# Stick-breaking attention in a hybrid trunk: VectorE and GpSimd swap the token tiles that they multiply, and the three passes of the value product change places

## The chip, the cores and the metric

The kernel runs on one core of one Trainium2 chip. The metric is the device time of one execution in microseconds. The kernel before was timed in three runs: 2732.86 us is the median, 2730.51 us the fastest and 2734.73 us the slowest. The profile comes from one further execution, with a time of its own.

The engines are named as in the profile: PE is TensorE's matmuls, PEld its weight loads, DVE is VectorE, ACT ScalarE, POOL GpSimd, and SP the queue that issues most transfers. L545 is line 545 of the kernel.

## The reference

One layer of a decoder is computed for 2048 tokens of width 1024, with 16 learned tokens put in front. The normed input is projected to some 9,200 columns. Three mixers with 4 heads of 128 read these: a stick-breaking attention, a gated delta rule and a gated linear recurrence (HGRN2). Each mixer's output is gated, projected back, gated again and summed; an output projection and the residual follow. The change touches the attention only:

```python
z = einsum('bhqd,bhkd->bhqk', q, k) * scale
log_keep = where(mask, log_sigmoid(-z), 0.0)
log_passed = cumsum(log_keep, axis=3, reverse=True) - log_keep
attn = where(mask, exp(log_sigmoid(z) + log_passed), 0.0)
out = einsum('bhqk,bhkd->bhqd', attn, v)
```

A key's weight is thus the sigmoid of its score, times the product, over all keys between it and the query, of the sigmoids of the negated scores. That running product, taken from the newest key back to the oldest, is what the kernel calls the remainder.

## The kernel before, in words

The sequence is cut into four quarters (j = 0 to 3) of 512 tokens, and a quarter into four token tiles (i = 0 to 3) of 128. For each quarter there is dense work (projections, branch products, output projection: `dense_work`) and there are scans (the attention head by head in `sb_scan`, then the delta rule in `gdn_mats` and `gdn_scan`, then HGRN2 in `hg_scan`). A matrix product in fp32 precision is split in three: both operands are held as a high part and a low part, and `mm3` (L175) adds three passes in PSUM, high by high, high by low, low by high (L176, L177, L178). One such pass over 512 columns is one MATMUL.

`weave` (L1427) runs a scan and the dense work as two generators and takes steps from one and the other by fixed numbers of microseconds. That sets the order in which the program is written. The framework's own scheduler (`schedule_with_timeline_sim`, L1610) then sets the final order on each engine from its estimate of times, so a change in one place can shift the order of other instructions. Each engine runs its instructions strictly in that order, and waits on semaphores.

The attention of one head and one quarter works down the keys' blocks, newest first, in two generators that `alternate`.

- `weights` (L519) goes through the four token tiles. For each: three passes on PE give the scores z; ACT takes two sigmoids (L533, the remainder's factor `pc`; L534, the weight's factor `at`); POOL sets or copies one column (L536, L538); DVE forms the running product with a TENSOR_TENSOR_SCAN (L539); and L545 multiplies `at` by `pc`. The engine of L545 alternates: tiles 0 and 2 on DVE, tiles 1 and 3 on POOL.
- `values` (L549) takes the finished block: PE transposes the products of all four tiles (L567) into one PSUM tile, ACT copies that as the high part `ath` (L578; L572 and L574 for the 16 learned tokens), DVE subtracts to get the low part `atl` (L127, a helper that other code uses as well), and `product` (L551) adds three passes into the accumulator `av`: values high by weights high, values high by weights low, values low by weights high. For the learned tokens it is one pass (L556).

At the end of a head `put_ob` (L407, L410) multiplies by the gate and splits the result. Most small tiles come from one ring of 21 buffers called S, so a buffer's next use waits for the last reader of its earlier use. The saved keys and values of older quarters are loaded through SP (L601 to L606), on the queue that loads weights too (L149).

The delta rule's products (L864), its block inverse on DVE (L923, L928), a transpose (L936) and its small matmuls on PE (L952, L973, L976) follow the attention of a quarter. Lines after L558 stand three lower in the changed file: L567 is L570 there, and L952 is L955.

Of the kernel before, what the change touches and what calls it, by code (L numbers as in the profile page):

```python
# [39 lines left out]
def kernel(  # L40
# [21 lines left out]
    nc = tc.nc  # L62
# [21 lines left out]
    def slot(tag, shape=(P, WQ), dt=F32, bufs=None):  # L84
        return pool.tile(list(shape), dt, tag=tag, name=nm(tag), bufs=bufs or BUFS[tag])
# [18 lines left out]
    def p_z():  # L104
        return ps_z.tile([P, 512], F32, tag="z", name=nm("z"))

    def p_tr():
        return ps_z.tile([P, 512], F32, tag="z", name=nm("tr"))

    def p_av():  # L110
        return ps_av.tile([P, 512], F32, tag="av", name=nm("av"))
# [14 lines left out]
    def sub_lo(out_, a, hi, eng=None):  # L126
        (eng or nc.gpsimd).tensor_sub(out_, a, hi.bitcast(F32))  # L127
# [47 lines left out]
    def mm3(dst, lh, ll, rh, rl, first, last):  # L175
        nc.tensor.matmul(dst, lh, rh, start=first, stop=False)  # L176
        nc.tensor.matmul(dst, lh, rl, start=False, stop=False)  # L177
        nc.tensor.matmul(dst, ll, rh, start=False, stop=last)  # L178
# [226 lines left out]
    def put_ob(src_ps, gate):  # L405
        t = slot("S")
        nc.vector.tensor_mul(t[:, META:], src_ps, gate[:, META:])  # L407
        oh = slot("ob", (P, TQ), F32R)
        ol = slot("ob", (P, TQ), F32R)
        nc.scalar.copy(oh, t[:, META:])  # L410
        sub_lo(ol, t[:, META:], oh)
        return oh, ol
# [99 lines left out]
    def sb_scan(j, h, st):  # L512

        qh, ql, kh, kl, vh, vl, vm0, rq, gate = st.pop(h)
        av = p_av()
        carry = [None] * NT
        started = [False]

        def weights(s, lo, hi, skh, skl, ats):  # L519
            for i in range(NT):  # L520
                e = min(hi, META + (i + 1) * P) if s == j else hi
                if e <= lo:
                    continue
                n = e - lo
                z = p_z()
                diag = s == j and e == META + (i + 1) * P
                qs = slice(META + i * P, META + (i + 1) * P)
                mm3(z[:, :n], qh[:, qs], ql[:, qs], skh[:, lo:e], skl[:, lo:e], True, not diag)
                if diag:
                    nc.tensor.matmul(z[:, n - P : n], ident_b, neg_b, start=False, stop=True)  # L530
                pc = slot("S")
                at = slot("S")
                nc.scalar.activation(pc[:, :n], z[:, :n], AF.Sigmoid, scale=rq[:, NT + i : NT + i + 1])  # L533
                nc.scalar.activation(at[:, :n], z[:, :n], AF.Sigmoid, scale=rq[:, i : i + 1])  # L534
                if carry[i] is None:
                    nc.gpsimd.memset(pc[:, n : n + 1], 1.0)  # L536
                else:
                    nc.gpsimd.tensor_copy(pc[:, n : n + 1], carry[i][:, 0:1])  # L538
                nc.vector.tensor_tensor_scan(  # L539
                    pc[:, 0:n][:, ::-1], pc[:, 0:n][:, ::-1], zero1.broadcast_to([P, n]),  # L540
                    1.0 if carry[i] is None else pc[:, n : n + 1], ALU.mult, ALU.add,
                )
                carry[i] = pc
                eng = nc.gpsimd if i % 2 else nc.vector
                eng.tensor_mul(at[:, :n], at[:, :n], pc[:, 1 : n + 1])  # L545
                ats[i] = at
                yield 0.4 + n * 0.0045

        def values(s, work, svh, svl, vm, final):  # L549
            def product(wi, ath, atl):  # L550
                lo, ats, a, kw, kt = work[wi]  # L551
                cs_ = slice(kt if (s == j and kt is not None) else 0, None)
                cs_ = slice(cs_.start * P, TQ)
                last = final and wi == len(work) - 1
                if kt is None:
                    nc.tensor.matmul(av, vm, ath[:96], start=not started[0], stop=last)  # L556
                else:
                    lh, ll = svh[:, kt * P : (kt + 1) * P], svl[:, kt * P : (kt + 1) * P]  # L558
                    mm3(av[:, cs_], lh, ll, ath[:, cs_], atl[:, cs_], not started[0], last)
                started[0] = True  # L560

            left = None
            for wi, (lo, ats, a, kw, kt) in enumerate(work):
                i0 = kt if (s == j and kt is not None) else 0
                tr = p_tr()
                for i in range(i0, NT):
                    nc.tensor.transpose(tr[:kw, i * P : (i + 1) * P], ats[i][:, a - lo : a - lo + kw], ident)  # L567
                ath = slot("S", (P, TQ), F32R)
                if kt is None:

                    atl = None
                    nc.scalar.copy(ath[:32], tr[:32])  # L572
                    sub_lo(ath[32:64], tr[:32], ath[:32], nc.vector)
                    nc.scalar.copy(ath[64:96], tr[:32])  # L574
                else:
                    atl = slot("S", (P, TQ), F32R)
                    cs_ = slice(i0 * P, TQ)
                    nc.scalar.copy(ath[:, cs_], tr[:, cs_])  # L578
                    sub_lo(atl[:, cs_], tr[:, cs_], ath[:, cs_], nc.vector)
                if left:  # L580
                    product(*left)
                left = (wi, ath, atl)
                yield 0.7
            product(*left)
            yield 0.1

        before = None
        work = []
        for s in range(j, -1, -1):
            vm = vm0  # L590
            if s == j:
                skh, skl, svh, svl = kh, kl, vh, vl
            else:
                cs = 0 if s == 0 else META
                skh = slot("S", dt=F32R)
                skl = slot("S", dt=F32R)
                svh = slot("S", (P, TQ), F32R)
                svl = slot("S", (P, TQ), F32R)
                dd = d_kv[(s, h, "k")] + d_kv[(s, h, "v")]
                for t_, d_ in ((skh, dd[0]), (skl, dd[1])):  # L600
                    nc.sync.dma_start(t_[:, cs:].bitcast(F32), d_[:, cs:])  # L601
                for t_, d_ in ((svh, dd[2]), (svl, dd[3])):
                    nc.sync.dma_start(t_.bitcast(F32), d_)
                if s == 0:
                    vm = slot("vmp", (96, HD), F32R, 2)
                    nc.sync.dma_start(vm.bitcast(F32), dd[4])  # L606
            for lo, hi in [(META + 2 * P, WQ), (0, META + 2 * P)] if s == 0 else [(META, WQ)]:
                ats = {}
                now = weights(s, lo, hi, skh, skl, ats)
                if before is None:  # L610
                    yield from now
                else:
                    yield from alternate(now, before)
                if lo == 0:
                    work.append((lo, ats, 0, 32, None))
                for kt in range(NT):
                    if lo <= META + kt * P < hi:
                        work.append((lo, ats, META + kt * P, P, kt))
                if s == j == 0 and lo > 0:
                    continue  # L620
                if s == j:
                    work.sort(key=lambda w_: -1 if w_[4] == 0 else (0 if w_[4] is None else w_[4]))
                before = values(s, work, svh, svl, vm, lo == 0)
                work = []
        yield from before
        return put_ob(av, gate)
# [708 lines left out]
    def alternate(*gens):  # L1335
        live = list(gens)
        while live:
            for g_ in list(live):
                c = next(g_, None)
                if c is None:  # L1340
                    live.remove(g_)
                else:
                    yield c
# [271 lines left out]
```

## Time and profile before

| | |
|---|---|
| median of three runs | 2732.86 us |
| the profiled execution: its time | 2729.9 us |
| the profiled execution: its span, first to last instruction | 2728.1 us |
| mean granted TensorE clock | 0.999 |
| matmuls, and weight loads | 17984 each |
| L545 on DVE | 108 instructions, median 442 ns |
| L545 on POOL | 108 instructions, median 673 ns |

The span is 1.8 us shorter than the execution's time, and that time is 3.0 us below the median of the three runs. A group in the profile reads: line, engine, operation, output and inputs by name, shape, count, then busy time and mean duration, then the idle time of the engine just before and what ended it. Wait rows give total, number and longest wait in microseconds. Matmuls overlap: each lasts about 0.4 us by the profile's model, but the next one starts 0.23 us after the one before.

### The profile page before, as it was taken

How to read it: one execution, taken by the hardware profiler on the slowest of the kernel's cores; microseconds unless marked ns; L12 is line 12 of the kernel's file. 1: busy time of each engine (PE TensorE's matmuls, PEld its weight loads, DVE VectorE, ACT ScalarE, POOL GpSimd, SP SyncE). 2: the span in 40 equal slices, each digit the busy share in tenths (PEclk: the TensorE clock that was granted, in tenths of full speed). 3: DMA queues.
4: the chain of work that ended last, by engine and by line, in shares of the span. 5: the costliest groups of instructions: out<-in, count | busy, mean ns of one | idle time of the engine just before them, and what ended most of it. 6: DMA issues, size and time to landing. Idle time of an engine off the chain costs nothing.

```text
span 2728.1 us, 46691 instructions
## 1 busy us (share of the span) xinstructions
PE 2690.0 (99%) x17984; PEld 2243.4 (82%) x17984; DVE 1432.5 (53%) x2870; ACT 961.0 (35%) x2199; POOL 717.7 (26%) x989
## 2 busy tenths in 40 slices
PE   7999999999999999999999999999999999999999
PEld 6998888888888888888888888888888887787887
DVE  5476647645357734443255765554325568556422
ACT  5564343343346212212144641321214456313120
POOL 4555213433133401112122332111212223302111
PEclk9999999999999999999999999999999999999999
DMA  7667756679554654557755456355774454554556
GB/s 263 221 234 251 256 178 221 231 268 320 195 180 146 205 177 130 157 158 241 231 190 171 156 168 205 106 158 155 248 221 140 163 168 143 164 161 122 160 163 213
DMA packets 200834, 521.08 MB, mean 191 GB/s; under 512 B 42848, under 2 KB 44832, under 8 KB 200612
## 3 DMA queue, kind: packets, MB, share of 16 engines
q1 hardware_dynamic: 200324, 518.03, 59.0%
q8 instruction: 142, 2.33, 0.3%
q14 instruction: 80, 0.66, 0.1%
q10 hardware_dynamic: 288, 0.07, 0.0%
HBM read 397.57 MB, written 120.44 MB: 190 GB/s over the span
## 4 chain that ended last, share of the span: by engine, by line
PE 92%; DVE 5%; DMA 1%; ACT 1%; issue 1%; POOL 0%; SPq 0%; DVEq 0%; ACTq 0%; POOLq 0%
PE acc L176 20%; PE acc L177 20%; PE acc L178 20%; PE av L176 5%; PE av L177 5%; PE av L178 5%; PE tr L567 2%; PE t L389 2%; PE z L1160 1%; PE z L176 1%; PE z L177 1%; PE z L178 1%; PE z L864 1%; PE tr L389 1%; PE tr L1245 1%
## 5 line engine op out<-in xcount | busy, mean ns | idle before, releaser
L176 PE MATMUL acc<-xh,w 128*128 128x512 f32 (+2 forms) x2096 | 796.8, 380 | 5.6 <-DVE y L1293 1.7
L177 PE MATMUL acc<-xl,w 128*128 128x512 f32 (+2 forms) x2096 | 790.0, 377 | 0.3 <-DVE xl L269 0.2
L178 PE MATMUL acc<-xh,w 128*128 128x512 f32 (+2 forms) x2096 | 786.7, 375 | 0.0
L176 PEld LDWEIGHTS acc<-xh,w 128*128 128x128 f32 x2096 | 396.1, 189 | 75.2 <-DVE y L1293 2.2
L178 PEld LDWEIGHTS acc<-xh,w 128*128 128x128 f32 x2096 | 396.4, 189 | 66.2 <-issue 0.2
L177 PEld LDWEIGHTS acc<-xl,w 128*128 128x128 f32 x2096 | 395.9, 189 | 65.2 <-DVE xl L269 1.3
L539 DVE TENSOR_TENSOR_SCAN S<-S,zero 128x128 f32<-128x128 f32 (+4 forms) x216 | 196.7, 913 | 113.8 <-ACT S L533 107.1
L127 POOL TENSOR_TENSOR w<-wraw,w 128x512 fp32r<-128x512 f32 x106 | 147.3, 1392 | 239.9 <-ACT w L156 222.4
L545 POOL TENSOR_TENSOR S<-S,S 128x256 f32<-128x256 f32 (+2 forms) x108 | 96.5, 894 | 367.1 <-DVE S L539 190.7
L176 PE MATMUL av<-xh,w 128*128 128x512 f32 (+2 forms) x440 | 172.7, 392 | 0.0
L177 PE MATMUL av<-xl,w 128*128 128x512 f32 (+2 forms) x440 | 171.9, 391 | 0.0
L178 PE MATMUL av<-xh,w 128*128 128x512 f32 (+2 forms) x440 | 171.3, 389 | 0.0
L156 ACT CAST w<-wraw 128x512 fp32r<-128x512 f32 x182 | 112.6, 619 | 142.4 <-PE acc L178 70.9
L533 ACT ACTIVATE S<-z,rq 128x128 f32<-128x128 f32 (+4 forms) x216 | 117.3, 543 | 117.7 <-PE z L178 90.2
L745 DVE SCALAR_TENSOR_TENSOR D<-D,cw,D 128x512 f32<-128x512 f32 (+1 forms) x144 | 119.0, 833 | 21.3 <-ACT D L743 19.8
L127 DVE TENSOR_TENSOR S<-tr,S 128x512 fp32r<-128x512 f32 (+4 forms) x176 | 105.9, 607 | 42.7 <-ACT S L572 24.0
L1297 POOL TENSOR_TENSOR y<-y,g 128x512 f32<-128x512 f32 x32 | 48.2, 1507 | 288.9 <-DVE g L1295 288.9
L176 PE MATMUL acc<-ob,w 128*128 128x512 f32 x296 | 118.0, 399 | 1.4 <-ACT ob L410 1.4
L177 PE MATMUL acc<-ob,w 128*128 128x512 f32 x296 | 117.7, 398 | 0.0
L178 PE MATMUL acc<-ob,w 128*128 128x512 f32 x296 | 117.6, 397 | 0.0
L534 ACT ACTIVATE S<-z,rq 128x128 f32<-128x128 f32 (+4 forms) x216 | 117.0, 542 | 0.0
L133 POOL TENSOR_SCALAR nu<-nv 128x8 f32<-128x8 f32 (+3 forms) x39 | 14.8, 379 | 334.2 <-DVE nv L1065 193.6
(407 smaller groups left out, 4978.2 us busy)
## 6 DMA issues: line engine op xcount, KB each, us to landing
w<-wk SPq DMA_DIRECT2D x555, 512.0 KB, 3.7
wk<-w SPq DMA_DIRECT2D x184, 512.0 KB, 3.5
wraw<-in_w_in_dram SPq DMA_DIRECT2D x142, 256.0 KB, 4.0
D<-in_xq_dram SPq DMA_DIRECT2D x56, 256.0 KB, 4.6
S<-rows SPq DMA_DIRECT2D x48, 256.0 KB, 5.2
S<-dv SPq DMA_DIRECT2D x48, 256.0 KB, 4.8
out_dram<-D SPq DMA_DIRECT2D x32, 256.0 KB, 4.6
S<-dk SPq DMA_DIRECT2D x24, 264.0 KB, 3.9
```

What stands on the lines that cost most here:

```text
L127: (eng or nc.gpsimd).tensor_sub(out_, a, hi.bitcast(F32))
L156: nc.scalar.copy(hi, raw)
L176: nc.tensor.matmul(dst, lh, rh, start=first, stop=False)
L177: nc.tensor.matmul(dst, lh, rl, start=False, stop=False)
L178: nc.tensor.matmul(dst, ll, rh, start=False, stop=last)
L389: nc.tensor.transpose(pt[:, n * P : (n + 1) * P], src[:, META + n * P : META + (n + 1) * P], ident)
L533: nc.scalar.activation(pc[:, :n], z[:, :n], AF.Sigmoid, scale=rq[:, NT + i : NT + i + 1])
L534: nc.scalar.activation(at[:, :n], z[:, :n], AF.Sigmoid, scale=rq[:, i : i + 1])
L539: nc.vector.tensor_tensor_scan(pc[:, 0:n][:, ::-1], pc[:, 0:n][:, ::-1], zero1.broadcast_to([P, n]), 1.0 if carry[i] is None else pc[:, n ...
L545: eng.tensor_mul(at[:, :n], at[:, :n], pc[:, 1 : n + 1])
L567: nc.tensor.transpose(tr[:kw, i * P : (i + 1) * P], ats[i][:, a - lo : a - lo + kw], ident)
L745: nc.vector.scalar_tensor_tensor(dst[:, c0:], raw[:, c0 + i : c0 + i + n], cw[:, ci, i : i + 1], dst[:, c0:], ALU.mult, ALU.add)
```

## The change

Two edits. In `weights` the engines of L545 are swapped: tiles 0 and 2 are multiplied on POOL, tiles 1 and 3 (the second and the fourth) on DVE. In `product` the call of `mm3` is written out, with its second and third pass exchanged, so that the pass that reads the weights' low part `atl` is the last of the three. Nothing else in the source differs.

```diff
-                eng = nc.gpsimd if i % 2 else nc.vector
+                eng = nc.vector if i % 2 else nc.gpsimd
                 eng.tensor_mul(at[:, :n], at[:, :n], pc[:, 1 : n + 1])
...
-                    mm3(av[:, cs_], lh, ll, ath[:, cs_], atl[:, cs_], not started[0], last)
+
+                    nc.tensor.matmul(av[:, cs_], lh, ath[:, cs_], start=not started[0], stop=False)
+                    nc.tensor.matmul(av[:, cs_], ll, ath[:, cs_], start=False, stop=False)
+                    nc.tensor.matmul(av[:, cs_], lh, atl[:, cs_], start=False, stop=last)
```

The first place is DVE's order at the end of the last head of the last quarter, as a piece of the difference (- before, + after). S_23435 and S_23451 are the running products of tiles 2 and 3 in the last block of keys, S_23436 and S_23452 the weights that they are multiplied into, S_23407 that of tile 1; tr is a PSUM tile of transposed weights.

```order
 L539 SCALAR_TENSOR_TENSOR S_23406<-S_23406,zero_383 128x272
+L545 TENSOR_TENSOR S_23407<-S_23407,S_23406 128x272
 L127 TENSOR_TENSOR S_23419<-tr_23413,S_23418 128x512
 L539 SCALAR_TENSOR_TENSOR S_23435<-S_23435,zero_383 128x272
 L539 SCALAR_TENSOR_TENSOR S_23451<-S_23451,zero_383 128x272
-L545 TENSOR_TENSOR S_23436<-S_23436,S_23435 128x272
+L545 TENSOR_TENSOR S_23452<-S_23452,S_23451 128x272
 L127 TENSOR_TENSOR S_23465<-tr_23460,S_23465 32x512
 L127 TENSOR_TENSOR S_23477<-tr_23471,S_23476 128x512
```

DVE now multiplies tile 3 behind that tile's own scan, and tile 2's multiplication, which stood there, has gone to POOL.

The second place is PE's order in the third quarter, where the delta rule's small matmuls begin. acc and av are accumulators of dense work here, ob the outputs of the attention's heads, z the small matmuls' output. Before:

```order
L178 MATMUL acc_18356<-ob_16520,w_3551_18337 128x512
L176 MATMUL av_18385<-ob_14962,w_3552_18339 128x512
L177 MATMUL av_18385<-ob_14963,w_3552_18339 128x512
L178 MATMUL av_18385<-ob_14962,w_3552_18339 128x512
L176 MATMUL av_18385<-ob_15493,w_3552_18339 128x512
L177 MATMUL av_18385<-ob_15494,w_3552_18339 128x512
L952 MATMUL z_17786<-S_17769,S_16847 32x32 x8
L952 MATMUL z_17786<-S_17769,S_17048 32x32 x8
```

After:

```order
L178 MATMUL acc_18011<-xh_14198,w_3475_18009 128x512
L389 MATMUL t_18130<-ident,D_17842 128x128 x4
L176 MATMUL acc_18176<-ob_14962,w_3406_17466 128x512
L177 MATMUL acc_18176<-ob_14963,w_3406_17466 128x512
L955 MATMUL z_17786<-S_17769,S_16847 32x32 x8
L955 MATMUL z_17786<-S_17769,S_17048 32x32 x8
```

Between the end of the rows after and the L952 of the rows before lie 51 dense passes: the small matmuls stand 51 passes earlier in PE's order than they did. The delta rule's products of that quarter (L864) stand 51 to 59 passes earlier as well. In the second quarter L864 moves by 0 to 27 passes and L952 not at all, in the fourth L864 by 0 to 2, in the first neither moves.

## The prediction

> **What bounds the kernel now.** I read the page first: the busy shares, with the number of instructions, and the forty slices.
>
> ```profile
> span 2728.1 us, 46691 instructions
> PE 2690.0 (99%) x17984; PEld 2243.4 (82%) x17984; DVE 1432.5 (53%) x2870; ACT 961.0 (35%) x2199; POOL 717.7 (26%) x989
> PE   7999999999999999999999999999999999999999
> ```
>
> PE is busy for 2690.0 of 2728.1 us, and only the first of the forty slices is below nine tenths. The change touches DVE and POOL, which are busy for 53% and 26%, and the order of PE's work, not its amount. At most 38.1 us of idle PE are there to be won, so the next views are those that say where this idle time lies: the busy time by stretches, for the four attention stages one below the other (the columns are the stretch, its length, then busy time and instructions of PE, PEld, DVE, ACT and POOL, the granted clock, the DMA share and GB/s), then PE's waits, of the whole span (first two rows), of 2080 to 2350 us (six rows) and of 1600 to 2080 us (five rows, of which the first and the last).
>
> ```profile
> 58.00:170.00 112.00, 111.97 (x788) 103.02 (x787) 53.57 (x104) 64.87 (x150) 60.35 (x83) 1.00 0.70 236
> 690.00:860.00 170.00, 170.00 (x905) 142.07 (x904) 95.44 (x166) 85.39 (x186) 49.20 (x94) 1.00 0.56 178
> 1370.00:1600.00 230.00, 230.00 (x1202) 191.40 (x1200) 145.33 (x233) 122.99 (x258) 63.41 (x127) 1.00 0.50 165
> 2080.00:2340.00 260.00, 255.72 (x1331) 210.43 (x1329) 173.22 (x270) 143.44 (x294) 73.24 (x131) 1.00 0.46 147
> ```
>
> ```profile
> PE acc L230 <- DVE D L221: 11.9, 1, 11.9
> ...
> PE acc L176 <- DMA w<-wk: 0.9, 2, 0.6
> ...
> PE av L556 <- ACT S L574: 2.0, 1, 2.0
> PE acc L176 <- DVE y L1293: 1.7, 1, 1.7
> PE acc L176 <- ACT ob L410: 1.4, 1, 1.4
> PE tr L567 <- DVE S L545: 0.8, 1, 0.8
> PE t L389 <- ACT D L767: 0.7, 1, 0.7
> PE av L177 <- DVE S L127: 0.7, 2, 0.5
> ...
> PE z L1160 <- DVE S L1151: 1.4, 1, 1.4
> ...
> PE z L1037 <- DVE r L1035: 0.2, 1, 0.2
> ```
>
> In three of the four attention stages PE is idle for 0.03 us in all, since dense passes fill every gap; a sooner weight there wins nothing. The fourth, where dense work runs out, has 4.28 us idle up to 2340. The largest single wait, 11.9 us, is the kernel's start and has no attention in it. All that this change can reach are the six rows of the fourth quarter (7.3 us) and, since the delta rule moves in PE's order, the five of the third (2.6 us): 9.9 us.
>
> **The passes.** Matmuls have 17984 weight loads, one each (the page gives PE and PEld the same count), so a changed order of passes saves no load and adds none: 0. What it does is put the low part's reader one pass later. The only place where PE waited for the low part is this, in two rows of the timeline:
>
> ```profile
> 2254.46 0.50 PE L177 MATMUL av<-S,S 128*128 128x512 f32 x1 [0.46 <-DVE S L127]
> ...
> 2257.68 0.50 PE L177 MATMUL av<-S,S 128*128 128x512 f32 x1 [0.23 <-DVE S L127]
> ...
> 1699.62 0.39 PE L178 MATMUL acc<-ob,w 128*128 128x512 f32 x1
> 1699.85 0.39 PE L176 MATMUL av<-ob,w 128*128 128x512 f32 x1
> ```
>
> The last two rows give the distance of passes: 0.23 us. The pass by the values' low part, long loaded, now fills 0.23 us of each wait. Of 0.46 and 0.23 us this takes 0.23 + 0.23, about 0.5 us. Bounds: 0.7 us, if the new order around it removes the waits altogether, and 0. What is late next is the same subtraction, 0.23 us short. The values' low part is wanted one pass sooner, but it comes with the high part's load well before.
>
> **The engines, by amount.** The multiplications by shape:
>
> ```profile
> L545 DVE TENSOR_TENSOR S<-S,S 128x512 f32<-128x512 f32 x24 | 16.5, 689 | 1.8
> L545 DVE TENSOR_TENSOR S<-S,S 128x272 f32<-128x272 f32 x28 | 12.2, 438 | 2.0
> L545 DVE TENSOR_TENSOR S<-S,S 128x256 f32<-128x256 f32 x24 | 10.2, 424 | 2.1
> ...
> L545 POOL TENSOR_TENSOR S<-S,S 128x512 f32<-128x512 f32 x36 | 40.7, 1130 | 106.4 <-DVE S L539 63.8 <-ACT S L533 10.3 <-ACT D L439 8.2
> L545 POOL TENSOR_TENSOR S<-S,S 128x256 f32<-128x256 f32 x40 | 32.9, 824 | 165.5 <-ACT S L533 60.8 <-DVE S L539 59.6 <-ACT D L426 13.8
> L545 POOL TENSOR_TENSOR S<-S,S 128x272 f32<-128x272 f32 x32 | 22.9, 716 | 95.2 <-DVE S L539 67.3 <-ACT D L740 7.9 <-ACT S L533 6.7
> ```
>
> DVE takes over POOL's 36, 40 and 32: 36 x 0.689 + 40 x 0.424 + 32 x 0.438 = 55.8 us. It gives up the three DVE rows (38.9 us) and 32 smaller ones. By shape those are 12 of 384 columns and 20 of 128 or 144; between 0.42 and 0.69 us the first, up to 0.42 us the second, so 5 to 17 us. DVE thus gains 0 to 12 us of work over four stages in which it is idle for half the time or so. POOL gets 24 x 1.130 + 28 x 0.716 + 24 x 0.824 = 66.9 us and at most 32 x 1.130 = 36.2 us for the small ones, against 96.5 us now. Cover: the dense passes, which keep PE at 100% in three stages. Cost: 0; what it costs without the cover is the next term.
>
> **The tail of the last head.** Here the cover is gone, and the chain shows:
>
> ```profile
> 2333.97 1.46 DVE L539 TENSOR_TENSOR_SCAN S<-S,zero 128x272 f32<-128x272 f32 x2 [0.40 <-POOL S L538]
> ...
> 2335.35 0.42 DVE L545 TENSOR_TENSOR S<-S,S 128x272 f32<-128x272 f32 x1
> 2335.61 0.69 POOL L545 TENSOR_TENSOR S<-S,S 128x272 f32<-128x272 f32 x1 [1.55 <-DVE S L539]
> 2335.82 1.03 PE L567 MATMUL tr<-ident,S 128*32 128x128 f32 x6 [0.77 <-DVE S L545]
> ...
> 2338.85 0.50 PE L556 MATMUL av<-S,vmp 96*128 96x512 f32 x1 [2.00 <-ACT S L574]
> ```
>
> DVE scans tiles 2 and 3 one behind the other, to 2335.43, then multiplies tile 2 to 2335.77; POOL multiplies tile 3 from 2335.61 to 2336.30, 0.18 us after the scan's end. PE transposes tile 2, then tile 3, and the wait of 2.00 us lies down the same chain. After the change POOL can begin tile 2 after its scan, half of 1.46 us in: 2333.97 + 0.73 + 0.18 = 2334.88, to 2335.57. DVE multiplies tile 3 from 2335.35 to 2335.77. Both are done by 2335.8, not 2336.3: 0.5 us sooner for all that follows. That is one bound. The other comes from two rows of the second quarter in which the engines got into each other's way:
>
> ```profile
> 757.23 1.76 DVE L539 TENSOR_TENSOR_SCAN S<-S,zero 128x256 f32<-128x256 f32 x2
> 758.09 1.34 POOL L545 TENSOR_TENSOR S<-S,S 128x256 f32<-128x256 f32 x1 [14.04 <-ACT S L533]
> ...
> 759.55 1.54 DVE L545 TENSOR_TENSOR S<-S,S 128x384 f32<-128x384 f32 x1 [0.55 <-POOL S L545]
> ...
> 1459.93 0.64 POOL L545 TENSOR_TENSOR S<-S,S 128x256 f32<-128x256 f32 x1
> ```
>
> The same multiplication on POOL takes 0.64 us alone and 1.34 beside a scan. If POOL's tile 2 is held up until the scan of tile 3 ends, it runs from 2335.43 to 2336.12, and if DVE's tile 3 then waits for POOL, it ends at 2336.54: 0.2 us later than now. I take 0.3 us sooner, nearer the first bound, since in this very place the two multiplications overlapped at 0.42 and 0.69 us, about their means. POOL's queue behind a blocked multiplication holds the column copies of the next block (L538), for which the next scans on DVE wait; at the tail there is no next block. Here stands a rule against the change. The Trainium skill, page "SBUF — State Buffer", section "Who interferes with whom", says that a VectorE instruction with two inputs in SBUF and a GpSimd instruction that reads SBUF exclude each other, and the one that comes second blocks in full. The pair of 1.34 and 0.64 us agrees with that; by the rule the term would be 0.2 us lost, not 0.3 won, and the sum below -0.3 us.
>
> **What else moves.** The order shows the third quarter's delta rule 51 dense passes earlier on PE. Its five waits (2.6 us) may shrink; bounds 2.6 us won and 0, and I take 0, since the rows after it keep their order. On SP's queue loads of keys and values pass up to three weight loads in the third and fourth quarter. A weight half that comes too late costs at most the time from issue to landing:
>
> ```profile
> w<-wk SPq DMA_DIRECT2D x555, 512.0 KB, 3.7
> ```
>
> I take 0, because PE waited for such loads for 0.9 us in 2728; the bound is 3.7 us lost.
>
> **The sum.** -0.5 - 0.3 = -0.8 us. Against the profiled execution's 2729.9 us that is 2729.1. The median of the runs lies 3.0 us above that execution, so the forecast for the median is 2732.86 - 0.8 = 2732.1 us. Bounds: -0.7 - 0.5 - 2.6 = -3.8 us, and +0.2 + 3.7 = +3.9 us: 2729.1 to 2736.8; the runs before lay 2.4 below and 1.9 above their median. About 0.2%, 5.5 us, is what a measurement of this kernel can tell from no change.
>
> **The rivals.**
>
> *Faster: the exposed waits go.* If the tail of the last head gets its cover back, the 9.9 us above are the limit. A gain of over 5.5 us needs more than half of them. For it: the six rows lie in one dependent stretch, and one sooner step shortens several. Against: the 1.4 and 1.7 us wait for `put_ob` and the branch product behind the head, which the change leaves as they are. All of it: 2723.0 us. Chance 0.06.
>
> *Slower: PE reaches the delta rule before VectorE does.* The place is the third quarter:
>
> ```profile
> 1697.35 0.71 DVE L936 STREAM_TRANSPOSE S<-S 128x512 f32<-128x512 f32 x1 [2.11 <-DMA S<-ud]
> ...
> 1701.08 1.20 PE L952 MATMUL z<-S,S 32*32 32x32 f32 x64
> ```
>
> PE runs in order, and L952 now stands 51 x 0.23 = 11.7 us earlier. Its input was ready at 1698.06, 3.0 us ahead. If the chain before it (row loads, inverse, transfer) does not start sooner, PE stands still for 8.7 us, dense passes queued behind, and the median becomes 2732.86 - 0.8 + 8.7 = 2740.8 us. It decides once that chain comes less than about 2.4 us sooner. Against: the order moves L864, the chain's head, by 51 to 59 passes too. Chance 0.06.
>
> *Slower: the blocked multiplications use up the cover.* By the pair above a blocked multiplication on POOL is 0.7 us late, and after the change both of POOL's tiles are followed by a scan on DVE, where before tile 3's was followed by the next block's at the earliest. There are 108 / 2 = 54 multiplications that are newly exposed. To lose 5.5 us beyond the forecast's gain 9 of them must reach PE: about 2739.2 us. Against: POOL's mean of 0.824 us for 256 columns shows that many are blocked today, and PE waited for a multiplication once, for 0.8 us. By the Trainium skill's rule above (page "SBUF — State Buffer") all 54 would be blocked, which decides nothing while the passes cover them. Chance 0.05.
>
> **The chances.** The forecast's own case has the rest, 0.83. Same is that case, faster the first rival (0.06), slower the other two (0.06 + 0.05 = 0.11). The range reaches from the forecast's lower bound less the scatter, 2729.1 - 2.4 = 2726.7, to 2739, which takes in its upper bound, the scatter, and part of the slower cases.
>
> **What would show it.** Right: PE still near 2690 us busy, 17984 matmuls, and no idle in the attention of the second and third quarter; the 0.46 us wait at most halved or gone; POOL's last multiplication ahead of DVE's in the tail, and L556 (still that line) a few tenths sooner. Wrong: PE waits of several microseconds ahead of L955 in the third quarter, or many rows of PE L570 waiting for L545, or weight loads waited for.

## The result, and the profile after

The changed kernel is slower, by little but by more than the scatter: 2736.6 us is the median of ten runs (2734.1 to 2740.5), 2730.2 us that of ten runs of the kernel before on the same chip (2726.2 to 2734.7). The ratio is 1.0024, with a 95% interval of 1.0016 to 1.0033: some 6.4 us lost where the forecast had 0.8 won. The profiled execution took 2736.64 us.

The page of the changed kernel, the span, the busy shares and the row of PE's forty slices:

```profile
span 2734.9 us, 46689 instructions
...
PE 2694.3 (99%) x17984; PEld 2244.6 (82%) x17984; DVE 1430.8 (52%) x2870; ACT 959.1 (35%) x2199; POOL 714.4 (26%) x989
...
PE   7999999999999999999999999999999999999999
```

The amount of work is what it was: 17984 matmuls and loads, 2870 instructions on DVE. The span is 6.8 us longer (2728.1 before), and the page does not say where. The stretches do. The attention of the second and third quarter is as full as before:

```profile
690.00:860.00 170.00, 170.00 (x914) 142.14 (x913) 99.32 (x172) 87.45 (x192) 47.50 (x99) 1.00 0.54 175
1370.00:1600.00 230.00, 230.00 (x1208) 191.43 (x1207) 147.08 (x235) 122.63 (x257) 65.45 (x130) 1.00 0.52 165
```

The last quarter is not. Its four heads end with their products for the learned tokens (L556): at 2115, 2198, 2272 and 2339 us before, at 2111, 2191, 2273 and 2343 us after. The changed kernel is 7 us ahead at the second of these: 4 us already at the first, which is no more than the scatter of executions (the sixth experiment below has the same program up to there and came to it at 2116 us), and 2.5 us for 11 dense passes, at 0.23 us each, that it has put off. At the fourth, by which both have run the same 15139 matmuls, it is 4 us behind. The fourth head's stretch, before, then after (PE's busy time and its matmuls are the first two numbers behind the length):

```profile
2272.00:2339.00 67.00, 64.10 (x338) 52.04 (x337) 54.17 (x86) 42.96 (x92) 23.41 (x35) 1.00 0.47 149
```

```profile
2273.00:2343.00 70.00, 61.09 (x310) 47.34 (x308) 53.69 (x85) 42.05 (x88) 20.82 (x35) 0.99 0.40 127
```

PE does 28 matmuls fewer in 3 us more, and is idle for 8.9 us and not 2.9. The matmuls that are missing are dense work. The same stretches for tiles named acc alone, which are accumulators of dense passes, each of the third and fourth heads cut in half, before:

```profile
2198.00:2235.00 37.00, 26.16 (x100) 18.07 (x100) 0.00 (x0) 2.43 (x4) 1.00 0.59 182
2235.00:2272.00 37.00, 19.21 (x76) 13.98 (x76) 0.00 (x0) 1.85 (x3) 1.00 0.35 112
2272.00:2305.00 33.00, 21.97 (x88) 15.78 (x87) 0.00 (x0) 1.79 (x3) 1.00 0.54 184
2305.00:2339.00 34.00, 14.71 (x56) 9.80 (x54) 0.00 (x0) 1.88 (x3) 1.00 0.40 116
```

And after:

```profile
2191.00:2232.00 41.00, 26.43 (x105) 19.21 (x106) 0.00 (x0) 2.94 (x5) 1.00 0.53 169
2232.00:2273.00 41.00, 27.29 (x110) 19.80 (x108) 0.00 (x0) 1.74 (x3) 1.00 0.44 139
2273.00:2308.00 35.00, 18.70 (x75) 13.73 (x75) 0.00 (x0) 2.88 (x5) 1.00 0.49 161
2308.00:2343.00 35.00, 11.31 (x42) 7.59 (x42) 0.00 (x0) 0.60 (x1) 0.98 0.31 92
```

The third head has 215 dense passes beside it and not 176, the fourth 117 and not 144 (the stretches are cut at whole microseconds, so that a few passes more fall into them than the counts in PE's program below have). Dense work that covered the fourth head before has been spent on the third, which needed little of it. PE's waits of 2080 to 2350 us in the changed kernel, all of them:

```profile
PE tr L570 <- POOL S L545: 2.2, 2, 1.3
PE av L556 <- ACT S L577: 2.0, 1, 2.0
PE av L560 <- ACT S L581: 1.5, 2, 0.9
PE acc L176 <- ACT ob L410: 1.4, 1, 1.4
PE av L560 <- DMA w<-wk: 1.3, 1, 1.3
PE av L562 <- DVE S L127: 1.2, 3, 0.5
PE acc L176 <- ACT D L743: 0.7, 1, 0.7
PE z L176 <- ACT S L534: 0.5, 1, 0.5
PE t L389 <- ACT D L770: 0.2, 1, 0.2
```

They sum to 11.0 us in 13 waits; the six rows before held 7.3 us in 7. The 2.0 and 1.4 us at the end of the last head stand as they did; before's 1.7 us for y is only 0.3 us here, behind 2350 us. What is new lies earlier, around the start of the fourth head, where PE had waited for nothing before:

```profile
2278.92 0.33 PE L570 MATMUL tr<-ident,S 128*128 128x128 f32 x1 [1.33 <-POOL S L545]
...
2289.44 0.50 PE L560 MATMUL av<-S,D 128*128 128x512 f32 x1 [1.32 <-DMA w<-wk]
...
2299.26 0.33 PE L560 MATMUL av<-S,D 128*128 128x128 f32 x1 [0.87 <-ACT S L581]
...
2300.10 0.33 PE L562 MATMUL av<-S,D 128*128 128x128 f32 x1 [0.40 <-DVE S L127]
```

Four different releasers, one after the other: POOL's multiplication, a transfer, ACT's copy, DVE's subtraction. That every step of a chain is waited for in turn points to other work that is missing beside the chain and not to one slow step; the experiments test it.

Behind the last head the trace shows something else that before's did not show there: the clock.

```profile
2340.00:2344.00 4.00, 1.97 (x9) 1.51 (x10) 2.24 (x4) 2.11 (x4) 0.00 (x0) 0.74 0.91 221
2344.00:2348.00 4.00, 2.57 (x7) 1.56 (x6) 1.29 (x2) 0.62 (x1) 0.32 (x1) 0.50 0.11 41
2348.00:2352.00 4.00, 4.00 (x18) 3.81 (x18) 1.91 (x2) 0.00 (x0) 1.95 (x2) 0.50 0.00 0
2352.00:2356.00 4.00, 3.68 (x19) 2.79 (x18) 2.71 (x5) 1.14 (x4) 3.72 (x6) 0.98 0.41 68
```

PE had the half clock for some 10 us there; before's row to 2360 us, shown with the experiments, has 1.00. Whether that is part of the loss was one of the questions.

### The profile page after: what moved, and what is told of

It is laid out like the page before. It is cut to its first block, busy times and chain, and to the rows that moved or that the text cites. A ratio compares the mean times of both kernels' runs of the same rounds, so it can differ in the third digit from the quotient of the medians.

```text
span 2734.9 us, 46689 instructions
## 1 busy us (share of the span) xinstructions
PE 2694.3 (99%) x17984; PEld 2244.6 (82%) x17984; DVE 1430.8 (52%) x2870; ACT 959.1 (35%) x2199; POOL 714.4 (26%) x989
## 4 chain that ended last, share of the span: by engine, by line
PE 94%; DVE 4%; ACT 1%; issue 1%; DMA 0%; POOL 0%; SPq 0%; DVEq 0%; ACTq 0%; POOLq 0%
PE acc L176 20%; PE acc L177 20%; PE acc L178 20%; PE av L176 4%; PE av L177 4%; PE av L178 4%; PE tr L570 2%; PE t L389 2%; PE z L1163 1%; PE av L562 1%; PE z L176 1%; PE z L177 1%; PE av L561 1%; PE z L178 1%; PE av L560 1%; PE z L867 1%
## 5 line engine op out<-in xcount | busy, mean ns | idle before, releaser
L176 PE MATMUL acc<-xh,w 128*128 128x512 f32 (+2 forms) x2096 | 795.8, 380 | 4.7 <-DMA w<-wk 1.2
L177 PE MATMUL acc<-xl,w 128*128 128x512 f32 (+2 forms) x2096 | 788.6, 376 | 0.3 <-DVE xl L269 0.2
L178 PE MATMUL acc<-xh,w 128*128 128x512 f32 (+2 forms) x2096 | 786.3, 375 | 0.0
L176 PEld LDWEIGHTS acc<-xh,w 128*128 128x128 f32 x2096 | 395.7, 189 | 74.0 <-issue 2.2
L178 PEld LDWEIGHTS acc<-xh,w 128*128 128x128 f32 x2096 | 395.8, 189 | 66.3 <-issue 0.2
L177 PEld LDWEIGHTS acc<-xl,w 128*128 128x128 f32 x2096 | 395.3, 189 | 65.6 <-DVE xl L269 1.3
L539 DVE TENSOR_TENSOR_SCAN S<-S,zero 128x128 f32<-128x128 f32 (+4 forms) x216 | 203.0, 947 | 116.6 <-ACT S L533 88.7
L545 POOL TENSOR_TENSOR S<-S,S 128x128 f32<-128x128 f32 (+4 forms) x108 | 92.2, 854 | 392.3 <-DVE S L539 245.2
L176 PE MATMUL av<-xh,w 128*128 128x512 f32 (+2 forms) x440 | 172.8, 393 | 0.0
L177 PE MATMUL av<-xl,w 128*128 128x512 f32 (+2 forms) x440 | 171.8, 390 | 0.0
L178 PE MATMUL av<-xh,w 128*128 128x512 f32 (+2 forms) x440 | 171.2, 389 | 0.0
L176 PE MATMUL acc<-ob,w 128*128 128x512 f32 x296 | 118.9, 402 | 1.4 <-ACT ob L410 1.4
L177 PE MATMUL acc<-ob,w 128*128 128x512 f32 x296 | 117.8, 398 | 0.0
L178 PE MATMUL acc<-ob,w 128*128 128x512 f32 x296 | 117.7, 398 | 0.0
L570 PE MATMUL tr<-ident,S 128*128 128x128 f32 (+1 forms) x608 | 103.0, 272 | 2.2 <-POOL S L545 2.2
```

The lines of the kernel that those rows point to most:

```text
L539: nc.vector.tensor_tensor_scan(pc[:, 0:n][:, ::-1], pc[:, 0:n][:, ::-1], zero1.broadcast_to([P, n]), 1.0 if carry[i] is None else pc[:, n ...
```

## The experiments

The theory: the change costs nothing by itself. It gives the framework's scheduler other estimates of time, and the scheduler then spends the last quarter's dense work beside the third head and leaves the fourth bare; the waits that open there are the loss. The rivals: the new engines cost by themselves; the new order of passes does; or the half clock does. A dense pass is one of L176 to L178 into an accumulator of dense work; the numbers such as 225, 176, 140 count them in PE's program between the ends of the first, second, third and fourth head (before 225, 176, 140; after 214, 213, 117). Every ratio is to runs of the kernel before on the same chip, from 5 to 11 runs of the kernel and 15 to 32 of before. One row of each profile is shown, the stretch from 2080 to 2360 us: PE's idle time is its length, 280 us, less the first number behind it. Before, it is 7.4 us:

```profile
2080.00:2360.00 280.00, 272.56 (x1422) 224.37 (x1420) 182.59 (x282) 146.94 (x304) 83.28 (x147) 1.00 0.46 148
```

After, 11.4 us:

```profile
2080.00:2360.00 280.00, 268.60 (x1361) 218.44 (x1360) 177.33 (x276) 142.66 (x296) 75.17 (x141) 0.98 0.44 141
```

**1. The changed kernel, with the first two heads of the last quarter as before.** 225, 173, 143.

```diff
-                eng = nc.vector if i % 2 else nc.gpsimd
+                eng = nc.vector if bool(i % 2) == bool(j < nq - 1 or h > 1) else nc.gpsimd
...
+                    if j < nq - 1 or h > 1:
...
+                    else:
+                        mm3(av[:, cs_], lh, ll, ath[:, cs_], atl[:, cs_], not started[0], last)
```

> The changed kernel, with the first and second head of the last quarter as before (old engines, old pass order). The order of PE then has 143 dense passes between the third and the fourth head's L556, where before had 140 and the changed kernel has 117. Theory of the cover (the loss comes from the dense passes that moved from beside the fourth head to beside the third): the loss goes, time ratio to before 0.999 to 1.0007. Rival, the engines (POOL's blocked multiplications delay the third and fourth head, whatever the order): the loss stays, 1.0015 to 1.003.

```profile
2080.00:2360.00 280.00, 275.05 (x1413) 226.73 (x1412) 180.33 (x280) 143.91 (x297) 82.61 (x148) 0.98 0.47 149
```

Measured 2727.93 us, ratio 0.9992 (0.9983 to 1.0001), and 5.0 us idle. The loss is gone, though the third and fourth head, in which the waits lay, still have the new engines and passes.

**2. The kernel before, with the change in the first two heads of the last quarter alone.** 214, 212, 118. The edit is the first one turned round.

> The kernel before, with the change in the first and second head of the last quarter alone. 118 dense passes are left beside the fourth head, whose engines and passes are the old ones. Theory of the cover: all of the loss, 1.0015 to 1.003, with PE waits of some 10 us in the fourth head. Rival, the engines: no loss, 0.9993 to 1.0007, since heads three and four are untouched.

```profile
2080.00:2360.00 280.00, 268.31 (x1374) 218.70 (x1373) 179.88 (x278) 144.50 (x297) 78.49 (x141) 0.99 0.44 142
```

2736.67 us, ratio 1.0025 (1.0016 to 1.0034), 11.7 us idle: the whole loss, with the waits in heads that nothing changed.

**3 and 4. One edit alone, everywhere.** The third kernel has only the swapped engines (214, 211, 119), the fourth only the exchanged passes (213, 191, 138).

> The swap of engines alone, old pass order. 119 dense passes beside the fourth head. Theory of the cover: most of the loss, 1.0012 to 1.003. Rival, the order of the passes: 0.9993 to 1.0007.

> The new order of the passes alone, old engines. 138 dense passes beside the fourth head. Theory of the cover: no loss, 0.9993 to 1.0007. Rival, the order of the passes: 1.0015 to 1.003.

```profile
2080.00:2360.00 280.00, 268.35 (x1380) 219.55 (x1379) 179.47 (x279) 144.56 (x299) 76.89 (x141) 0.99 0.44 143
```

```profile
2080.00:2360.00 280.00, 273.33 (x1394) 223.51 (x1393) 179.45 (x279) 144.78 (x300) 84.16 (x145) 0.98 0.46 146
```

The swap: 2735.24 us, 1.002 (1.0011 to 1.0029), 11.7 us idle. The passes: 2729.94 us, 1.0002 (0.9993 to 1.001), 6.7 us idle. The order of passes falls as a cause.

**5. The kernel before, woven otherwise.** Neither an engine nor a pass is changed; the first head of the last quarter takes five chunks of dense work and not four, and the fourth head four and not five (the expectation names only the first). 213, 207, 118.

```diff
-            obs[0, h] = weave(sb_scan(j, h, sst), sb_us, 4 + (h == H - 1))
+            obs[0, h] = weave(sb_scan(j, h, sst), sb_us, (5, 4, 4, 4)[h] if j == nq - 1 else 4 + (h == H - 1))
```

> The kernel before, with its engines and its order of passes, in which only the first head of the last quarter's attention is woven with five chunks of dense work at each step and not four. In PE's program the stretches that end with the last product of the second, third and fourth head then hold 213, 207 and 118 dense passes (before 225, 176, 140; changed kernel 214, 213, 117). Theory of the cover: as slow as the changed kernel, ratio 1.0015 to 1.003 to the kernel before, with 9 to 13 us of PE waiting between 2180 and 2360 us, though neither an engine nor a pass has been changed. Rival, the loss is tied to the new engines or passes themselves: 0.9993 to 1.0007.

The row to 2360 us, and the accumulators of dense work in the two halves of the fourth head:

```profile
2080.00:2360.00 280.00, 266.43 (x1355) 216.29 (x1354) 178.40 (x276) 144.71 (x297) 75.75 (x139) 0.99 0.44 140
...
2279.00:2313.00 34.00, 19.13 (x77) 13.92 (x76) 0.00 (x0) 2.33 (x5) 1.00 0.48 164
2313.00:2348.00 35.00, 11.18 (x42) 7.59 (x42) 0.00 (x0) 1.15 (x3) 1.00 0.33 95
```

2741.71 us, ratio 1.0042 (1.003 to 1.0055), 13.6 us idle. The direction is the theory's, the size is more than it said. The fourth head's 77 and 42 passes are the changed kernel's 75 and 42: the loss needs no new engine.

**6. The changed kernel, with idle transposes ahead of the last product.** They fill the last wait of the last head and compute nothing that is used.

```diff
+                if j == nq - 1 and h == H - 1 and final and wi == len(work) - 1:
+                    fl = p_tr()
+                    for _ in range(16):
+                        nc.tensor.transpose(fl[:, :P], ats[NT - 1][:, :P], ident)
```

> The changed kernel with 16 transposes more on PE, of a tile that has long been there into a tile that nobody reads, between the last transpose and the last product of the last head, where the changed kernel's PE waits. They compute nothing that is used and bring no wait forward; they only keep PE busy, some 2 us at 0.13 us each. Theory with a share for the clock: the stretch of half clock behind that wait (2340 to 2352 us) goes, PEclk stays 1.00 there, and of the loss of 6.5 us 2 to 4 us are won back: ratio 1.0008 to 1.0018 to the kernel before. Rival, the half clock costs nothing, or is the consequence of something else than idle PE: 1.0022 to 1.0035, no faster than the changed kernel.

```profile
2346.00:2350.00 4.00, 3.01 (x18) 2.10 (x15) 2.45 (x5) 1.28 (x3) 0.00 (x0) 1.00 0.69 191
2350.00:2356.00 6.00, 3.87 (x26) 3.27 (x26) 3.45 (x5) 1.76 (x5) 3.07 (x5) 1.00 0.13 29
```

The clock stayed at 1.00 behind the last head, and the median shows no gain: 2736.43 us, 1.0024 (1.0013 to 1.0034). My number for the clock's share failed. In the profiled executions the part from the fourth head's L556 to the end is 2.2 us shorter with the full clock (2737.2 - 2347.35 = 389.8 us, the changed kernel 2734.9 - 2342.86 = 392.0); a share of that size is within the intervals. But the loss is not the clock's. With a mean clock of 0.999 the kernel before took 2728.99 us (median of 25 of its runs beside all experiments) and the changed one 2736.06 (3 runs); at 0.998 it was 2729.75 (28) and 2737.52 (5). At equal clock 7 to 8 us are lost. And the rows of the first and fourth experiment have the 0.98 of the changed kernel without its loss.

The Trainium skill, page "TensorE: Matmul & The Clock Gate", section "Why this matters for your kernels", advises against PE idle gaps of over about 3 us between bursts of matmuls, since one window of idle brings the half clock. Here it fell where no single gap was over 2.0 us, so in this trace shorter gaps were enough. Such gaps do not decide it alone: the kernel before had waits of 0.8, 2.0 and 1.4 us in the same place and kept 1.00, while the ninth experiment, with the same order of matmuls from 2080 us to there and the same three waits, had 0.66 from 2337 to 2341 us. So it is not shown that it was the transposes that kept the clock at 1.00.

**7 and 8. Products that wait go last.** At the end of the last head the accumulators of dense work hold products that wait for that very head (the wait of 1.4 us for ob). In the last two quarters they were put behind the gates' products, in the changed kernel (214, 213, 171) and in the kernel before (225, 176, 194).

```diff
-            yield from take(b0, 3 if ahead else 5)
+            if not ahead:
+                yield from take(b0, 5)
             yield from gdn_gates(j, xs, range(H), gst)
-            if not ahead:
-                yield from take(b0, 3)
+            yield from take(b0, 3)
```

> The changed kernel, in which the dense work of the last two quarters issues the three first heads' output products (take of branch 0) behind the gates' products and not ahead of them. The two PSUM tiles of the dense work are then not held by products that wait for the fourth head while that head is computed, and the stretch of the last head has 171 dense passes instead of 117 in PE's program, 24 of them right ahead of its last product. Theory of the cover: the waits of the last head shrink from 11 us to under 6, and the loss is gone: 0.997 to 1.0. Rival, the loss needs the old engines: 1.002 to 1.003 as the changed kernel.

> The same edit on the kernel before (194 dense passes in the last head's stretch, before 140). Theory of the cover: the waits of 2200 to 2350 us, 7 us before, shrink to 2 to 5 us, and the time is that of the changed kernel with this edit to within 3 us: 0.997 to 1.0. Rival, the engines matter once the cover is equal: the two kernels with the edit differ by over 3 us. Other rival, the gates come sooner at the price of a wait elsewhere: 1.0 to 1.003.

For the seventh, the last head and what comes behind it:

```profile
2080.00:2360.00 280.00, 272.08 (x1389) 222.46 (x1388) 175.67 (x274) 144.53 (x297) 67.82 (x131) 0.99 0.43 144
2360.00:2720.00 360.00, 352.73 (x2703) 291.18 (x2702) 162.33 (x399) 68.13 (x193) 69.60 (x86) 0.98 0.55 167
```

Two misses. The seventh took 2740.88 us, 1.004 (1.0027 to 1.0054), the eighth 2733.18 us, 1.0015 (1.0006 to 1.0024). The idle time up to 2360 us fell by 3.5 us in each (to 7.9 and 4.0), and came back behind: 7.3 us from 2360 to 2720 us in the seventh and 7.1 in the eighth, where before has 2.3 and the changed kernel 2.7. It is the delta rule's chain (L955, L976, L995 and L1009 of the seventh, five waits of 4.9 us in all from 2441.8 to 2452.2 us) that now runs bare, and PE had about half the clock behind its start: 0.53 from 2444 to 2462 us in the seventh, 0.51 from 2434 to 2451 us in the eighth. How much of the time of these two is the clock's was not separated. The dense work is one fixed amount: what covers the last head is missing beside the next chain. The two kernels also differed by 7.7 us and not by under 3; but their cover differs too (171 and 194), so that said nothing of the engines.

**9 to 12.** The ninth has the change in the first three quarters alone (225, 176, 140), the tenth the late products on the first experiment's kernel (225, 173, 197), and the last two put one of the three products back ahead of the gates, on the changed kernel (214, 213, 156) and on the first experiment's (225, 173, 182). The edit of these last two, against the changed kernel:

```diff
-            yield from take(b0, 3 if ahead else 5)
+            yield from take(b0, 1 if ahead else 5)
             yield from gdn_gates(j, xs, range(H), gst)
-            if not ahead:
-                yield from take(b0, 3)
+            yield from take(b0, 2 if ahead else 3)
```

> The change in the first three quarters' attention alone; the last quarter as in the kernel before, where the stretches of the second, third and fourth head hold 225, 176 and 140 dense passes as before. Theory of the cover: nothing is lost and next to nothing won, ratio 0.9993 to 1.0007, since those three stages had no idle PE. Rival, the new engines win something in these quarters that the changed kernel's last quarter hides (the kernel with the old engines in the first two heads of the last quarter stood at 0.9992): 0.998 to 0.9992.

> The late output products (the three of branch 0 behind the gates in the last two quarters) on the kernel that has the new engines and passes in every head but the first two of the last quarter. The last head's stretch has 197 dense passes, with the new engines; 194 with the old ones gave a ratio of 1.0015, 171 with the new ones 1.004. Theory of the cover: as the old engines with 194, 1.0005 to 1.0025. Rival, the engines of the last head cost something by themselves: 1.003 to 1.005.

> The changed kernel, in which one of the three output products stays ahead of the gates and two go behind them (last two quarters). The last head's stretch has 156 dense passes and not 117; the delta rule's chain, which waited 5 us at 2440 to 2452 us where all three went behind, stands 15 passes (some 3.5 us) later than there. Theory of the cover, with the dense work as a fixed amount that covers either the last head or the chain behind it: between the changed kernel and before, 0.9995 to 1.0025. Rival, every shift of dense work out of its written order costs: 1.003 to 1.0045.

> The same edit (one product ahead of the gates, two behind) on the kernel with the old engines in the first two heads of the last quarter; 182 dense passes beside the last head. If the waits at the end of the last head (4.9 us in that kernel) go and the chain behind it stays covered, the fastest of all: 0.9970 to 0.9985. If the chain's waits come as in the kernels with three late products: 0.9995 to 1.002.

The ninth: 2728.85 us, 0.9992 (0.9983 to 1.0001), 7.4 us idle to 2360 us as in before. Three quarters with the new engines cost nothing; whether they win 0.1% stays open. The tenth: 2731.41 us, 1.0008 (0.9999 to 1.0016). With the new engines in the last head and 197 passes it is no slower than the old engines with 194 (1.0015): the rival that the engines cost by themselves in that head falls. The eleventh missed: 2741.61 us, 1.0043 (1.0031 to 1.0056). The twelfth: 2732.86 us, 1.0012 (1.0004 to 1.0021). In both, one product ahead of the gates did not spare the chain behind them; the stretch behind the last head holds 7.7 us idle in the twelfth:

```profile
2360.00:2720.00 360.00, 352.28 (x2690) 290.54 (x2689) 158.77 (x395) 65.42 (x186) 65.82 (x80) 0.98 0.56 167
```

By then all kernels slower by 0.2% or more had 207 to 213 passes beside the third head, so it could be that head as well as the fourth, and every kernel with the new engines in all heads was among them.

**13. The changed kernel, with the cover back.** Engines and passes are the changed kernel's in every head. Only the price of a step of attention, by which dense work is woven in, is 1.6 times as high in the last quarter, so that `weave` takes less dense work per step and leaves more for the end of each head. 199, 212, 142.

```diff
         sb_us = 4 * (2.0 + 2.7 * j) + 0.8 * (5 + 4 * j)
+        sb_us *= 1.6 if j == nq - 1 else 1.0
```

> The changed kernel with its engines and its order of passes in every head of every quarter; only the price of a step of attention, by which dense work is woven in, is multiplied by 1.6 in the last quarter. In PE's program the stretches of the second, third and fourth head then hold 199, 212 and 142 dense passes (changed kernel 214, 213, 117; before 225, 176, 140), and among the fourth head's other matmuls they lie nearly as in the kernel with the old engines in the first two heads. Theory of the cover of the fourth head: the waits of 2255 to 2310 us (4.8 us in the changed kernel) fall to under 1.5, and the loss is gone: 0.9985 to 1.0008. Rival, the engines and passes in the first two heads cost by themselves, or the third head's 212 passes do: 1.0015 to 1.003.

The row to 2360 us, and the dense accumulators in the two halves of the fourth head:

```profile
2080.00:2360.00 280.00, 273.97 (x1431) 227.06 (x1430) 181.19 (x282) 143.55 (x297) 84.39 (x149) 0.99 0.48 153
...
2264.00:2297.00 33.00, 22.21 (x87) 15.20 (x86) 0.00 (x0) 1.80 (x3) 1.00 0.56 190
2297.00:2331.00 34.00, 16.03 (x61) 10.85 (x59) 0.00 (x0) 1.86 (x3) 1.00 0.42 122
```

Its waits from 2080 to 2350 us, all of them:

```profile
PE av L556 <- ACT S L577: 2.0, 1, 2.0
PE acc L176 <- DVE y L1296: 1.7, 1, 1.7
PE acc L176 <- ACT ob L410: 1.4, 1, 1.4
PE tr L570 <- POOL S L545: 0.9, 1, 0.9
```

2724.71 us, ratio 0.9988 (0.9979 to 0.9997): the loss is gone, and this kernel is faster than the kernel before by 0.03 to 0.21%, and so than the changed one as well. The fourth head has 87 and 61 passes, near before's 88 and 56, in place of 75 and 42, and the waits at its start have vanished, all four. The third head has 212 passes and the first two the new engines: neither is the cause.

So the cause is shown from both sides: the cover taken away by the weave alone brings the loss (fifth), the cover given back by the weave alone takes it away (thirteenth). The two edits' part in it is that the swap, not the passes, leads to the order that strips the fourth head. Why the scheduler chooses that order is not shown; its estimates are in no trace.

**How the loss adds up.** From the first head's L556 to the fourth's PE runs 1130 matmuls before and 1132 after. The kernel before takes 2338.85 - 2115.43 = 223.4 us for them, the changed one 2342.86 - 2111.13 = 231.7, which is 8.3 us more. The kernels without the loss and with as many matmuls there are near the former (221.6 us in the first experiment, 225.1 in the fourth, 223.5 in the ninth), those with it near the latter (232.1 in the second, 231.2 in the third). By the rows of waits PE's idle time in that stretch rises from 4.2 us in 5 waits to 9.6 in 12. A row of waits counts from the modelled end of the matmul before, some 0.4 us after its start, while dense passes start 0.23 us apart: each wait is thus 0.17 us longer than its row says, and with 7 more waits that is an estimate of 1.2 us. So 5.4 + 1.2 = 6.6 of the 8.3 us are waits; the remaining 1.7 stay open. Behind the fourth head the changed kernel's execution is 2.7 us longer (392.0 and 389.3), where it had the half clock, and up to the first it was 4.3 us shorter, the scatter told above; together that is the 6.8 us of the spans, to the rounding. The medians are 6.4 us apart, and their interval (4.4 to 9.0) takes in the 8.3.

## Why the prediction was wrong

The sign was wrong, and same had 0.83. That the time lay within the range (2726.7 to 2739), and even just under the sum's upper bound of 2736.8, is luck: the forecast started from 2732.86 us, the median of three runs, and ten runs of the same kernel have 2730.2. The loss of 6.4 us lies outside the sum's bounds of -3.8 and +3.9.

**The step that failed** is the sentence "All that this change can reach are the six rows of the fourth quarter (7.3 us) and, since the delta rule moves in PE's order, the five of the third (2.6 us): 9.9 us". It took the waits that there were as all that a change could touch. The reordering opened waits where there had been none: four at the start of the fourth head, 3.9 us by their rows, out of 5.4 us more idle time from the first head's end to the fourth's. I had compared the moved instructions of the delta rule in the third quarter and those of the last head's tail, and had not counted the dense passes beside each head of the last quarter, the only stage with idle time. That count (140 against 117) stood in the order of the two programs and would have told it.

**The passes**, -0.5 us (bounds -0.7 and 0). The waits at L177 of 0.46 and 0.23 us in the third head are gone, but three others for the same subtraction have come, 1.2 us. Alone, the exchanged passes measured 1.0002 (0.9993 to 1.001): a term of this size cannot be told from 0.

**The amount**, 0, held: DVE was busy for 1430.8 us after 1432.5, POOL for 714.4 after 717.7, and the attention of the second and third quarter kept PE full.

**The tail of the last head**, -0.3 us (bounds -0.5 and +0.2). The changed kernel's rows:

```profile
2338.07 1.45 DVE L539 TENSOR_TENSOR_SCAN S<-S,zero 128x272 f32<-128x272 f32 x2
...
2338.99 0.99 POOL L545 TENSOR_TENSOR S<-S,S 128x272 f32<-128x272 f32 x1 [3.23 <-DVE S L539]
...
2339.62 0.65 DVE L545 TENSOR_TENSOR S<-S,S 128x272 f32<-128x272 f32 x1
...
2340.03 0.83 PE L570 MATMUL tr<-ident,S 128*32 128x128 f32 x6 [0.89 <-POOL S L545]
...
2342.86 0.79 PE L556 MATMUL av<-S,vmp 96*128 96x512 f32 x1 [2.00 <-ACT S L577]
```

From the start of the scans to L556 it takes 4.79 us, and took 2338.85 - 2333.97 = 4.88. The chain is 0.1 us shorter, between the bounds. POOL did begin 0.92 us into the scans (0.91 by the prediction's working), but took 0.99 us beside the second where it had taken 0.69, and DVE 0.65 where it had taken 0.42. This is the rule of the Trainium skill that the prediction weighed (page "SBUF — State Buffer", section "Who interferes with whom"): the trace agrees that the two get in each other's way, but held up to the scans' end (2339.52) and then 0.69 us long, POOL's would have ended at 2340.21, and it ended at 2339.98, by the profile's rough times of POOL: something less than a full block.

**Slower, PE reaches the delta rule first** (0.06): did not happen. L955 of the third quarter came 14.6 us sooner than L952 had (1686.44 and 1701.08), and waited for nothing; the chain ahead of it moved along, as the argument against had it.

```profile
1686.44 1.20 PE L955 MATMUL z<-S,S 32*32 32x32 f32 x64
```

**Slower, the blocked multiplications use up the cover** (0.05): the nearest rival, with the right shortage and the wrong cause. PE waited twice for a multiplication of POOL, 2.2 us in all, and not 9 times. The cover was not used up by slow multiplications; it was moved away. (Its time of 2739.2 us leaves out the forecast's gain: 2732.1 + 9 x 0.7 is 2738.4.)

**Transfers**, 0 (bound +3.7): one wait for the DMA queue, 1.3 us, in the bare stretch; with the cover back (thirteenth experiment) it is not there.

## What to carry to other kernels

Where a scheduler sets the order, count the filler beside each dependent chain before and after: which chain keeps how much of it matters more than what the edited instructions cost. Filler is a fixed amount, so a wait that is covered in one place can open in the next chain, and several waits in a row for different engines mean that the cover has gone and not that any of them is slow. When an edit loses for this reason, give the filler back through the weaving and time it again before dropping the edit.

## What the runs showed of the hardware

The clock behind the bare stretch was at half for some 10 us (rows 2340 to 2352 above) although no gap ahead of it was longer than 2.0 us and PE was busy for the whole of its last 4 us. The same waits did not always bring it: with 0.8, 2.0 and 1.4 us in that place the kernel before kept a clock of 1.00, and the ninth experiment fell to 0.66. With the half clock the part behind the fourth head took 392.0 us in the changed kernel, and 389.8 us with the full clock in the sixth experiment, which has the same matmuls there.

POOL's multiplication of 128 x 272 took 0.99 us beside a scan on DVE, and 0.69 in the same place before, where it ran behind the scans (the profile's times of POOL are rough).
